# PEER gates in two passes of 64 expert rows instead of three, with gates stored ahead of the activations, in a two-layer encoder kernel

## The chip, the cores and the metric

The kernel runs on one core of a Trainium2 chip. The metric is the device time of one execution in microseconds (us); each figure below is a median of three executions, or one execution that the hardware profiler recorded. The engines are TensorE (PE in the rows; PEld is its weight load), VectorE (DVE), ScalarE (ACT), GpSimd (POOL) and SyncE (SP), which issues most DMA transfers.

## What is computed

Two encoder layers on 256 tokens of width 1024. Each layer is a token mixer (two attention branches), which the change does not touch, and a PEER block, which it does:

```python
def peer_ffn(x, w_query, sub_keys, expert_down, expert_up):
    # per head, product-key top-k over 128 x 128 experts; expert e adds g_e * v_e * gelu(u_e . x)
    def chunk(xc):                                    # PEER_CHUNK = 128 tokens, two chunks
        q = (xc @ w_query).reshape(128, 8, 2, half)
        s = einsum('thpk,pnk->thpn', q, sub_keys)
        sv, si = top_k(s, 16)
        cand = ...                                    # 16 x 16 sums and their expert numbers
        top_s, sel = top_k(cand, 16)
        eidx = take_along_axis(cidx, sel, axis=-1)    # 8 heads x 16 experts of each token
        g = softmax(top_s, axis=-1)
        u, vv = expert_down[eidx], expert_up[eidx]    # 16384 experts x 1024
        act = gelu(einsum('td,thkd->thk', xc, u))
        return einsum('thk,thkd->td', g * act, vv)
```

## The kernel before

**The PEER block as the kernel does it.** The 16384 experts are a grid of 128 rows i by 128 columns j. The kernel does not gather `expert_down`: it multiplies all 128 rows of it (one row is 128 experts, one *down unit*, D0 to D127, 24 matmuls of 256 columns) with all 256 tokens. Two units share a PSUM bank, the ScalarE applies Gelu to it, and the result stands in `act` (128 j, 128 i, 2 chunks, 128 tokens and one number). The *gates*, the softmax weights, are then multiplied into `act`, where an expert that a token did not pick gets zero. `expert_up` is read only where some token picked the expert: the rows of `act` are sorted into lists in DRAM, experts used by the first chunk alone, by both, by the second alone, and by none, and only the blocks of 128 experts up to a cap are read back, each with a gather of its 128 rows of `expert_up`. The other rows are taken whole, without sorting. A *block* is U0, U1, and so on; a block for one chunk is 6 matmuls of 512 columns, for both chunks 12.

**Precision.** Every weight tile `raw` is split into `wh` (ScalarE copy, L190) and `wl` (VectorE subtraction, L193), four of each in turn; a product is three matmuls. The copy of unit k+4 can start when TensorE is done with unit k. A block's slice of `act` is split too (L1214 and L1216), after the split of its `raw`.

**Lists.** `LISTS = [(0, 56, 46, 34, 11), (92, 36, 30, 22, 7)]` gives for each list its first row, its rows, and in blocks its cap, the end of the first chunk's and the start of the second chunk's. `WHOLE = (56, 36)` are the rows taken whole. `blocks_of` puts them in order: list 0, the whole rows, list 1.

**Gates.** `gate_lane` starts `gate_group` for each of the 32 groups of 8 tokens, in three passes, over the rows of list 0, the whole rows, and those of list 1 (`GATES`). A group builds on VectorE the one-hot rows `ej` (128 columns j, L1017), `ei` (w rows i, L1022) and `ag` (ei times the gate, in two halves, L1026), on ScalarE `el` (L1020), and on TensorE 16 matmuls per group for the gates (L1043) and, in the two passes of a list, 8 more that count which chunk uses which expert (L1039). VectorE then multiplies the gates from PSUM into `act` (L1053). This last step waits for the Gelu of the pass's last row, so the third pass cannot finish a group before all 128 rows are activated.

**From ranks to blocks.** When a pass of a list is through, `rank_lane` turns the counts into a place for every expert. `send_lane` then lets GpSimd write the list's rows out, one indirect DMA of 128 experts each (L1132), paced by waits on VectorE's splits: for list 0 every second send waits for a new split, for list 1 each. `read_back` (SyncE, L1169) reads a sorted block once all sends of its list have landed, and GpSimd gathers its `expert_up` rows (L1198).

**What sets the order.** Each engine runs a fixed order, written by `Lanes`: a planner that holds a clock for TensorE, VectorE and ScalarE and lets each lane (a Python generator) issue its next step when the planned time has come. TensorE's steps are the main loop; the gates, splits and Gelus are lanes that fill the other engines. The numbers in the `yield`s are planned costs. They order the instructions and do not hold them up on the chip, where only semaphores do.

## Time and profile before

| what | us |
|---|---|
| median of three executions (1909.34 to 1910.23) | 1909.83 |
| the profiled execution | 1909.23 |
| its span from first to last instruction | 1907.4 |
| down units of layer 1 on TensorE, first matmul to last | 247.1 to 657.7 |
| gates of layer 1 on TensorE | 400.1 to 767.6 |
| blocks of layer 1 on TensorE | 669.3 to 960.0 |
| down units of layer 2 | 1194.8 to 1605.4 |
| blocks of layer 2 | 1617.0 to 1903.2 |

All rows below are of the profiled execution. A row of the timeline starts with the start in us and the duration in us; "xN" is the number of like instructions merged into it, and a bracket tells how long the engine was idle before it and what ended that. Matmuls overlap, and so do instructions in a row on VectorE and ScalarE, so what one instruction costs its engine is the distance between two starts, which is less than its duration.

### The profile page before, as it was taken

Reading aid. Unit: us, or ns where it says so; the run is one execution under the profiler, and the core shown is the slowest. Engines: PE = TensorE matmul, PEld = TensorE weight load, DVE = VectorE, ACT = ScalarE, POOL = GpSimd, SP = SyncE. Lnnn points to the kernel's source line nnn. Section 1 sums busy time; section 2 is a strip of 40 time slices with the busy share of each in tenths; the row PEclk is TensorE's granted clock in tenths of the full one; section 3 lists DMA queues with packets and bytes.
Section 4 is the critical chain, followed back from the end, with each engine's and each line's share of the span. In section 5 each row is a group of like instructions: output and inputs, shape, how many; then the busy total and the mean of one; then the engine's idle time right before and its main releaser. Section 6 shows DMA issues by size and latency. Waiting matters only on the chain. (4 is left out here: it accounts for less than half of the span.)

```text
span 1907.4 us, 40308 instructions
## 1 busy us (share of the span) xinstructions
PE 1869.3 (98%) x15922; PEld 1695.4 (89%) x15922; DVE 1551.6 (81%) x3281; ACT 1109.0 (58%) x1550; POOL 383.6 (20%) x344
## 2 busy tenths in 40 slices
PE   8999999999999899999999999999999998999998
PEld 7889899999999878788778989999999998787886
DVE  6976899988988699755689778999889886996565
ACT  4665454556666577545646654455666665775454
POOL 0000000000054544335200000000000544534352
PEclk8999999999999999999999999999999998999999
DMA  7434455554467687877464354555544776778783
GB/s 254 155 110 159 155 177 190 177 176 145 155 207 222 214 261 233 269 235 263 163 230 140 110 179 141 178 184 182 168 149 148 222 220 228 249 239 259 205 291 129
DMA packets 122652, 370.74 MB, mean 194 GB/s; under 512 B 16080, under 2 KB 36432, under 8 KB 122448
## 3 DMA queue, kind: packets, MB, share of 16 engines
q1 hardware_dynamic: 91728, 264.00, 44.4%
q0 software_dynamic: 30720, 104.02, 15.5%
q8 instruction: 129, 2.11, 0.5%
q14 instruction: 75, 0.61, 0.1%
HBM read 342.60 MB, written 25.35 MB: 193 GB/s over the span
## 5 line engine op out<-in xcount | busy, mean ns | idle before, releaser
L190 ACT ACTIVATE wh<-raw 128x1024 fp32r<-128x1024 f32 x480 | 506.0, 1056 | 326.8 <-PE bank L1273 129.5
L193 DVE TENSOR_TENSOR wl<-raw,wh 128x1024 fp32r<-128x1024 f32 x480 | 582.0, 1219 | 135.9 <-ACT wh L190 132.9
L1272 PE MATMUL bank<-TT,wh 128*128 128x256 f32 x2048 | 585.3, 286 | 0.0
L1274 PE MATMUL bank<-TT,wl 128*128 128x256 f32 x2048 | 578.9, 283 | 0.0
L1273 PE MATMUL bank<-TT,wh 128*128 128x256 f32 x2048 | 578.6, 283 | 0.0
L1306 PE MATMUL bank<-wh,TT 128*128 128x512 f32 x1464 | 413.9, 400 | 7.5 <-PEq L1321 4.5
L1272 PEld LDWEIGHTS bank<-TT,wh 128*128 128x128 f32 x2048 | 387.3, 189 | 0.2
L1273 PEld LDWEIGHTS bank<-TT,wh 128*128 128x128 f32 x2048 | 386.0, 188 | 0.0
L1274 PEld LDWEIGHTS bank<-TT,wl 128*128 128x128 f32 x2048 | 385.2, 188 | 0.0
L1306 PEld LDWEIGHTS bank<-wh,TT 128*128 128x128 f32 x1464 | 273.2, 189 | 77.8 <-DVE TT L1216 8.2
L1132 POOL DMA_INDIRECT rows<-act,rank x184 | 199.1, 1082 | 512.4 <-DVE scr L1113 278.0
L1306 PE MATMUL bank<-wl,TT 128*128 128x512 f32 x732 | 232.6, 397 | 1.2 <-issue 1.2
L193 DVE TENSOR_TENSOR wl<-act,wh 128x1024 fp32r<-128x1024 f32 x132 | 161.2, 1223 | 82.1 <-ACT wh L190 80.0
L1020 ACT ACTIVATE el<-ej 128x1024 f16<-128x1024 f16 x192 | 193.5, 1046 | 57.1 <-DVE ej L1017 56.9
L190 ACT ACTIVATE wh<-act 128x1024 fp32r<-128x1024 f32 x132 | 139.3, 1057 | 107.3 <-PE bank L1306 103.2
L1224 ACT ACTIVATE act<-bank 128x512 f32<-128x512 f32 x128 | 76.6, 598 | 157.3 <-PE bank L1274 155.5
L1306 PEld LDWEIGHTS bank<-wl,TT 128*128 128x128 f32 x732 | 138.2, 189 | 33.4 <-DVE wl L193 0.3
L871 POOL IOTA act<- 128x128 uint32 x4 | 1.7, 437 | 804.6 <-PE bank L356 416.8
L1053 DVE TENSOR_TENSOR act<-act,bank 128x288 f32<-128x288 f32 (+1 forms) x192 | 93.3, 508 | 63.7 <-PE bank L1043 39.6
L436 PE MATMUL bank<-TT,wh 128*128 128x256 f32 x448 | 129.8, 290 | 1.5 <-ACT raw_ka L564 1.0
L438 PE MATMUL bank<-TT,wh 128*128 128x256 f32 x448 | 126.7, 283 | 0.0
L439 PE MATMUL bank<-TT,wl 128*128 128x256 f32 x448 | 126.5, 282 | 0.0
(249 smaller groups left out, 3039.9 us busy)
## 6 DMA issues: line engine op xcount, KB each, us to landing
raw<-in_downs_dram SPq DMA_DIRECT2D x256, 512.0 KB, 3.6
raw<-in_wts_dram SPq DMA_DIRECT2D x132, 512.0 KB, 3.7
act<-in_ups_dram SPq DMA_DIRECT2D x44, 512.0 KB, 4.9
raw<-in_ups_dram SPq DMA_DIRECT2D x28, 512.0 KB, 5.1
act<-rows SPq DMA_DIRECT2D x76, 129.0 KB, 3.8
act<-rows SPq DMA_DIRECT2D x76, 64.5 KB, 4.4
rows<-act,rank POOLq DMA_INDIRECT x184, 4.8
Sq<-in_rpb_dram SPq DMA_DIRECT2D x2, 876.0 KB
```

What stands on the lines that cost most here:

```text
L190: self.nc.scalar.activation(h, r, AF.Copy)
L193: self.splits.append(self.nc.vector.tensor_sub(lo, r, h.bitcast(F32)).ins.name)
L436: nc.tensor.matmul(o, wh, rh, start=first and i == 0 and pc == 0, stop=False, skip_group_check=True)
L438: nc.tensor.matmul(o, wh, rl, start=False, stop=False, skip_group_check=True)
L439: nc.tensor.matmul(o, wl, rh, start=False, stop=last and i == len(kcs) - 1 and pc == 1, skip_group_check=True)
L1020: nc.scalar.activation(el, ej, AF.Copy, scale=LOW)
L1053: nc.vector.tensor_mul(a, a, b[:, 0:8 * w].rearrange("p (t i) -> p i t", i=w))
L1132: snd = nc.gpsimd.indirect_dma_start(byrank[r], bass.IndirectOffsetOnAxis(ap=rank[:, i:i + 1], axis=0), afl[:, i * ROW:(i + 1) * ROW], None)
L1272: nc.tensor.matmul(o, lh, TT[:, :, 0, kc, :], start=kc == 0, stop=False)
L1273: nc.tensor.matmul(o, lh, TT[:, :, 1, kc, :], start=False, stop=False)
L1274: nc.tensor.matmul(o, ll, TT[:, :, 0, kc, :], start=False, stop=kc == 7)
L1306: nc.tensor.matmul(oacc[ch][hf], a, r[:, hf * 512:(hf + 1) * 512], start=first[hf] and a is lh and r is h, stop=last and a is ll)
```

## The change

1. **Two passes.** `GATES` is gone; `gate_group` now covers 64 rows in each of two passes, so 64 groups a layer in place of 96. A group has 16 gate matmuls of 64 columns (36 or 56 before) and always 8 counting matmuls, of 64 columns in the first pass (rows of list 0) and of 36 in the second (rows of list 1).
2. **Gates first or Gelu first.** A group no longer waits for the Gelu of its rows. Rows that are activated by then are multiplied on VectorE as before (L1059); for the rest the ScalarE stores the gates in `act` as they are (L1062). `gelu_lane` does the converse: for tokens whose gates are stored it applies Gelu in place in PSUM (L1244) and VectorE multiplies it into `act` (L1252), chunk by chunk; the other tokens are activated straight into `act` (L1249).
3. **Lists.** `LISTS = [(0, 64, 53, 39, 13), (92, 36, 30, 22, 7)]`, `WHOLE = (64, 28)`. A layer has 26 blocks for both chunks and 27 for one in list 0 (23 and 23 before), 28 whole rows (36), and list 1 as before: 180 products of a block with a chunk in place of 186, 111 splits in place of 112, 100 sends in place of 92.
4. **Sends.** Sends of list 0 are paced at 0.4 splits each and those of list 1 at 0.6; list 1 starts when every block of list 0 has been asked for. A send of list 0 no longer waits for the end of the gates of other rows, only for its own row and the rank.

```diff
-LISTS = [(0, 56, 46, 34, 11), (92, 36, 30, 22, 7)]
-WHOLE = (56, 36)
-GATES = [LISTS[0][:2] + (0,), WHOLE + (None,), LISTS[1][:2] + (1,)]
+LISTS = [(0, 64, 53, 39, 13), (92, 36, 30, 22, 7)]
+WHOLE = (64, 28)
...
+        cnts, counted, gates, gelus = {}, [0, 0], [0, 0], [0]
+
+        def gate_group(r, n, o):
...
+            i0, w = LISTS[r][:2]
+            p0 = 64 * r
...
             for t in range(8):
-                if r is not None:
-                    nc.tensor.matmul(cnts[r][:, (n // 16) * w:(n // 16 + 1) * w], ej[:, t // 2, :, t % 2],
...
+                nc.tensor.matmul(cnts[r][:, half * w:(half + 1) * w], ej[:, t // 2, :, t % 2],
+                                 ei[:, t // 2, i0 - p0:i0 - p0 + w, t % 2], start=counted[r] == 0 and t == 0,
+                                 stop=counted[r] == NG - 1 and t == 7, skip_group_check=True)
...
-            yield from lane_need([("gelu", (i0 + w) // 2 - 1)])
-            t = yield ("v", vcost(8 * w))
...
+            while gates[r] < n:
+                yield None
+            t = yield ("v", 0.35)
+            bv = b.rearrange("p (t i) -> p i t", i=64)
+            g = min(max(2 * gelus[0] - p0, 0), 64)
+            if g:
+                t = lanes.use("v", vcost(8 * g) - 0.35)
+                a = act[:, p0:p0 + g, half, t0:t0 + 8]
+                nc.vector.tensor_mul(a, a, bv[:, 0:g])
+            if g < 64:
+                t = max(t, lanes.use("s", scost(8 * (64 - g)), lanes.cur - 0.3))
+                nc.scalar.activation(act[:, p0 + g:p0 + 64, half, t0:t0 + 8], bv[:, g:64], AF.Copy)
...
         def send_lane(r):
...
-            yield from lane_need([("G", 2 * r), ("rank", r)])
+            yield from lane_need([("rank", r)])
+
+            while r and st.nd < up0 + len([x for x in seq if x[1] == 0]):
+                yield None
+            pace = len(st.splits) - 3.0
             for i in range(i0, i0 + w):
+                yield from lane_need([("row", i // 2)])
...
+                pace += (0.4, 0.6)[r]
...
         def gelu_lane(b, acc):
...
+            r, av = b // 32, acc.rearrange("p (a t) -> p a t", a=2)
+
+            g = 8 * gates[r]
+            if g:
+                nc.scalar.activation(av[:, :, 0:g], av[:, :, 0:g], AF.Gelu)
+            for c in range(2):
+                g0 = min(max(g - 128 * c, 0), 128)
+                a, ac = act[:, 2 * b:2 * b + 2, c], av[:, :, 128 * c:128 * c + 128]
+                if g0 < 128:
+                    nc.scalar.activation(a[:, :, g0:128], ac[:, :, g0:128], AF.Gelu)
+                if g0:
+                    t = max(t, lanes.use("v", vcost(2 * g0), lanes.cur))
+                    nc.vector.tensor_mul(a[:, :, 0:g0], a[:, :, 0:g0], ac[:, :, 0:g0])
```

**What it does to the order: VectorE in the second pass.** From the split of unit D110 to that of D112, before (L1017, L1022, L1026 build a group, L1053 multiplies gates into `act`):

```order
L193 TENSOR_TENSOR wl<-raw,wh 128x1024
L1022 TENSOR_TENSOR ei_2244<-iota_71,ijT 128x4x72
L1026 TENSOR_TENSOR ag_2246<-ei_2244,gT 128x4x72 x2
L1022 TENSOR_TENSOR ei_2245<-iota_71,ijT 128x4x72
L1026 TENSOR_TENSOR ag_2247<-ei_2245,gT 128x4x72 x2
L1053 TENSOR_TENSOR act<-act,bank_7694 128x36x8
L1053 TENSOR_TENSOR act<-act,bank_7699 128x36x8
L193 TENSOR_TENSOR wl<-raw,wh 128x1024
L1017 TENSOR_TENSOR ej_2240<-iota_71,ijT 128x1024
L1017 TENSOR_TENSOR ej_2241<-iota_71,ijT 128x1024
L193 TENSOR_TENSOR wl<-raw,wh 128x1024
```

and now, from the split of D109 to that of D111 (L1024, L1028 and L1019 build a group, L1059 multiplies gates into `act`, L1252 a Gelu from PSUM):

```order
L192 TENSOR_TENSOR wl<-raw,wh 128x1024
L1059 TENSOR_TENSOR act<-act,bank_7750 128x42x8
L1024 TENSOR_TENSOR ei_2244<-iota_71,ijT 128x512
L1028 TENSOR_TENSOR ag_2246<-ei_2244,gT 128x512 x2
L1019 TENSOR_TENSOR ej_2241<-iota_71,ijT 128x1024
L192 TENSOR_TENSOR wl<-raw,wh 128x1024
L1024 TENSOR_TENSOR ei_2245<-iota_71,ijT 128x512
L1028 TENSOR_TENSOR ag_2247<-ei_2245,gT 128x512 x2
L1252 TENSOR_TENSOR act<-act,bank_7774 128x2x88
L192 TENSOR_TENSOR wl<-raw,wh 128x1024
```

The multiplication of a fresh Gelu (L1252) now stands directly ahead of the split of D111; before, VectorE had no part in a Gelu.

**ScalarE at the same place**, before (L1020 makes `el`, L1224 is the Gelu of a bank, L190 the copy `wh`):

```order
L1020 ACTIVATE el_2242<-ej_2240 128x1024
L1020 ACTIVATE el_2243<-ej_2241 128x1024
L1224 ACTIVATE act<-bank_7275 128x4x128
L190 ACTIVATE wh<-raw 128x1024 x2
L1020 ACTIVATE el_2242<-ej_2240 128x1024
L1020 ACTIVATE el_2243<-ej_2241 128x1024
```

and now (L1022 makes `el`, L1062 stores gates, L189 is the copy `wh`):

```order
L189 ACTIVATE wh<-raw 128x1024
L1062 ACTIVATE act<-bank_7750 128x22x8
L1022 ACTIVATE el_2242<-ej_2240 128x1024
L189 ACTIVATE wh<-raw 128x1024
L1022 ACTIVATE el_2243<-ej_2241 128x1024
L1244 ACTIVATE bank_7774<-bank_7774 128x2x88
L1249 ACTIVATE act<-bank_7774 128x2x40
L1249 ACTIVATE act<-bank_7774 128x2x128
L189 ACTIVATE wh<-raw 128x1024
L1062 ACTIVATE act<-bank_7833 128x20x8
```

One Gelu has become three instructions. The second L1249 holds a wait for VectorE's L1252 on the same bank, and the copy `wh` of D111 stands right behind it.

**VectorE at the end of the down units**, before (the two last splits, then the third pass):

```order
L193 TENSOR_TENSOR wl<-raw,wh 128x1024 x2
L1053 TENSOR_TENSOR act<-act,bank_8605 128x36x8
L1053 TENSOR_TENSOR act<-act,bank_8610 128x36x8
L1053 TENSOR_TENSOR act<-act,bank_8874 128x36x8
L1053 TENSOR_TENSOR act<-act,bank_8875 128x36x8
L1017 TENSOR_TENSOR ej_2240<-iota_71,ijT 128x1024
L1017 TENSOR_TENSOR ej_2241<-iota_71,ijT 128x1024
L1022 TENSOR_TENSOR ei_2244<-iota_71,ijT 128x4x72
```

and now (from the split of block U0 to that of U2; L1229 splits a block's slice of `act`):

```order
L192 TENSOR_TENSOR wl<-raw,wh 128x1024
L1024 TENSOR_TENSOR ei_2245<-iota_71,ijT 128x512
L1028 TENSOR_TENSOR ag_2247<-ei_2245,gT 128x512 x2
L1059 TENSOR_TENSOR act<-act,bank_8864 128x62x8
L1019 TENSOR_TENSOR ej_2240<-iota_71,ijT 128x1024
L192 TENSOR_TENSOR wl<-raw,wh 128x1024
L1024 TENSOR_TENSOR ei_2244<-iota_71,ijT 128x512
L1028 TENSOR_TENSOR ag_2246<-ei_2244,gT 128x512 x2
L1059 TENSOR_TENSOR act<-act,bank_8941 128x62x8
L1252 TENSOR_TENSOR act<-act,bank_8931 128x2x128
L1252 TENSOR_TENSOR act<-act,bank_8931 128x2x72
L192 TENSOR_TENSOR wl<-raw,wh 128x1024
```

Before, the four multiplications behind the last split of a down unit waited for the last Gelu, with six groups of the third pass behind them; now the splits of the first blocks stand among the groups, and 7 groups are left for the time of the blocks, where 26 were.

## Rows read from the trace of the kernel before

**Rows 1.** The page, part 1: TensorE's matmuls, busy us, share, instructions.

```profile
PE 1869.3 (98%) x15922; PEld 1695.4 (89%) x15922; DVE 1551.6 (81%) x3281; ACT 1109.0 (58%) x1550; POOL 383.6 (20%) x344
```

**Rows 2.** Stretches: length, each engine's busy us, PEclk, DMA share, GB/s.

```profile
490.00:520.00 30.00, 30.00 (x378) 29.72 (x378) 26.65 (x48) 18.45 (x21) 0.00 (x0) 1.00 0.48 158
...
731.00:761.00 30.00, 30.00 (x297) 24.02 (x296) 29.73 (x63) 22.68 (x32) 14.13 (x12) 1.00 0.75 233
```

**Rows 3.** Timeline of TensorE: 24 matmuls of a down unit, 6 of a block.

```profile
329.88 0.28 PE L1272 MATMUL bank<-TT,wh 128*128 128x256 f32 x1
...
332.76 0.28 PE L1272 MATMUL bank<-TT,wh 128*128 128x256 f32 x1
...
800.78 1.10 PE L1306 MATMUL bank<-wh,TT 128*128 128x512 f32 x4
...
802.19 1.09 PE L1306 MATMUL bank<-wh,TT 128*128 128x512 f32 x4
```

**Rows 4.** Timeline of TensorE: first matmul of three gate bursts, first behind each.

```profile
485.52 0.20 PE L1039 MATMUL bank<-ei,ej 128*128 128x56 f16 x1
...
486.17 0.37 PE L1272 MATMUL bank<-TT,wh 128*128 128x256 f32 x1
...
567.47 0.19 PE L1043 MATMUL bank<-ag,ej 128*128 128x36 f16 x1
...
568.29 0.36 PE L1272 MATMUL bank<-TT,wh 128*128 128x256 f32 x1
...
711.36 0.20 PE L1039 MATMUL bank<-ei,ej 128*128 128x36 f16 x1
...
712.57 0.48 PE L1306 MATMUL bank<-wh,TT 128*128 128x512 f32 x1
```

**Rows 5.** Line L1306 from the last down unit: us, PE, PEld, PEclk, DMA, GB/s.

```profile
657.70:684.80 27.10, 13.57 (x48) 9.83 (x49) 0.81 0.83 296
1605.40:1633.10 27.70, 14.12 (x49) 10.25 (x50) 0.75 0.80 283
```

**Rows 6.** Timeline of VectorE: a group of the first pass, and the last down unit.

```profile
485.14 1.23 DVE L193 TENSOR_TENSOR wl<-raw,wh 128x1024 fp32r<-128x1024 f32 x1
486.37 0.62 DVE L1053 TENSOR_TENSOR act<-act,bank 128x448 f32<-128x448 f32 x1
486.91 0.38 DVE L1022 TENSOR_TENSOR ei<-iota,ijT 128x448 f16<-128x448 f16 x1
...
487.94 0.69 DVE L1017 TENSOR_TENSOR ej<-iota,ijT 128x1024 f16<-128x1024 f16 x1
488.54 1.22 DVE L193 TENSOR_TENSOR wl<-raw,wh 128x1024 fp32r<-128x1024 f32 x1
...
658.62 0.82 DVE L1053 TENSOR_TENSOR act<-act,bank 128x288 f32<-128x288 f32 x2 [9.35 <-ACT act L1224]
```

**Rows 7.** Timeline of ScalarE in the second pass.

```profile
596.50 1.06 ACT L190 ACTIVATE wh<-raw 128x1024 fp32r<-128x1024 f32 x1 [2.11 <-PE bank L1273]
597.46 1.99 ACT L1020 ACTIVATE el<-ej 128x1024 f16<-128x1024 f16 x2
```

**Rows 8.** Groups by line and shape: ScalarE, 256 elements; busy us, mean ns.

```profile
L1214 ACT ACTIVATE TT<-act 128x256 fp32r<-128x256 f32 x146 | 58.5, 400 | 0.0
```

**Rows 9.** Timeline of GpSimd: sends of list 0, then the first gather.

```profile
534.02 1.16 POOL L1132 DMA_INDIRECT rows<-act,rank  x1 [139.00 <-DVE scr L1113]
...
541.34 1.91 POOL L1132 DMA_INDIRECT rows<-act,rank  x1 [0.30 <-issue]
...
551.25 0.96 POOL L1132 DMA_INDIRECT rows<-act,rank  x1 [0.30 <-issue]
...
646.64 1.34 POOL L1132 DMA_INDIRECT rows<-act,rank  x1 [0.30 <-issue]
653.12 0.99 POOL L1198 DMA_INDIRECT raw<-in_ups_dram,act  x1 [5.14 <-DMA act<-rows]
```

**Rows 10.** The page, part 6: loads of whole rows, KB each, us to landing.

```profile
raw<-in_ups_dram SPq DMA_DIRECT2D x28, 512.0 KB, 5.1
```

More of the change, by code (lines that the diff above doesn't have):

```diff
@@ L1036, in gate_group @@
             yield ("p", 0.75)
+            half, t0 = n // 16, 8 * (n % 16)
             for t in range(8):
[L1038 to L1041 removed]
+                nc.tensor.matmul(cnts[r][:, half * w:(half + 1) * w], ej[:, t // 2, :, t % 2],
+                                 ei[:, t // 2, i0 - p0:i0 - p0 + w, t % 2], start=counted[r] == 0 and t == 0,
+                                 stop=counted[r] == NG - 1 and t == 7, skip_group_check=True)
@@ L1042, in gate_group @@
                 for k, e in enumerate((ej, el)):
-                    nc.tensor.matmul(b[:, t * w:(t + 1) * w], e[:, t // 2, :, t % 2],
+                    nc.tensor.matmul(b[:, t * 64:(t + 1) * 64], e[:, t // 2, :, t % 2],
                                      ag[:, k, t // 2, :, t % 2], start=k == 0, stop=k == 1)
-            counted[g] += 1
-            if counted[g] == NG and r is not None:
+            counted[r] += 1
+            if counted[r] == NG:
                 lanes.add(rank_lane(r, cnts[r]), after=lanes.cur)
@@ L1059, in gate_lane @@
+            if gates[r] == NG:
+                for k in range(32 * r, min(gelus[0], 32 * r + 32)):
+                    done["row", k] = t
         def gate_lane():
             yield from lane_need(["idx"])
-            for g in range(len(GATES)):
+            for r in range(2):
                 for n in range(NG):
                     o = yield from buf_take("oh")
-                    lanes.add(gate_group(g, n, o), after=lanes.cur)
+                    lanes.add(gate_group(r, n, o), after=lanes.cur)
@@ L1204, in split_rows @@
             if seq[n - up0][1] is None:
-                yield from lane_need([("G", 1)])
+                yield from lane_need([("row", seq[n - up0][2] // 2)])
             while n not in stage:
@@ L1222, in gelu_lane @@
         def gelu_lane(b, acc):
+            while gelus[0] < b:
+                yield None
             t = yield ("s", scost(512))
-            nc.scalar.activation(act[:, 2 * b:2 * b + 2, :, 0:HALF - 1],
-                                 acc.rearrange("p (a c t) -> p a c t", a=2, c=2), AF.Gelu)
+            r, av = b // 32, acc.rearrange("p (a t) -> p a t", a=2)
[10 more added lines that the diff above has]
+                    nc.vector.tensor_mul(a[:, :, 0:g0], a[:, :, 0:g0], ac[:, :, 0:g0])
+            lanes.cur = max(lanes.cur, t)
             give(acc, "a")
-            done["gelu", b] = t
+            gelus[0] += 1
+            if gates[r] == NG:
+                done["row", b] = t
         for ch in range(2):
```

43 lines of the change are left out of this document (15 added, 28 removed).

## The prediction

> **What bounds the kernel now.** I read the page's busy shares first: TensorE 1869.3 us, 98% of the span, VectorE 81%, ScalarE 58% [rows 1]. A busy TensorE can still be a waiting one, so next come the distances between its matmuls. A down unit's 24 matmuls take 2.88 us, 0.120 each, and a block's 6 take 1.41 us, 0.235 each [rows 3], and a gate group stands between two units without a hole [rows 4]. So from the first down unit to the last block TensorE's own work sets the time, and what leaves its queue leaves the time. There is one exception: at the end of the down units, 48 block matmuls and 8 gate groups need 27.1 us in layer 1 and 27.7 in layer 2 with the clock granted at 0.81 and 0.75 of full speed, part of it at the lower level [rows 5]. There VectorE sat 9.35 us behind the last Gelu [rows 6], its queue holding the third pass in order. Last the slack beside TensorE: VectorE is busy 26.65 of 30 us in the first pass, and 29.73 of 30 later among the blocks, still without holding TensorE up [rows 2].
>
> **Gates.** Bursts cost, from their first matmul to the first one behind [rows 4]: 24 matmuls at 56 columns 0.65 us (27.1 ns each), 32 at 36 columns (two groups) 0.82, 48 at 36 (two groups) 1.21. A layer has 32 groups of the first, 16 of the second, 16 of the third sort: 20.8 + 13.1 + 19.4 = 53.3 us. Now 64 groups of 24. At 64 columns the price is unseen; from 25.4 ns at 36 and 27.1 at 56 I go on to 27.7, with 25.4 (columns free) and 29.5 (the slope doubled) as ends. First pass 32 x 24 x 27.7 = 21.3; second, with 8 counting matmuls at 36 columns, 32 x (16 x 27.7 + 8 x 25.4) = 20.7; together 42.0. That removes 11.3 us per layer, 22.6 in all, 18 to 27 between the ends. All of it lies on TensorE's path.
>
> The rows show 25.4 ns at 36 columns and 27.1 at 56, a weak slope. [...]
>
> **Blocks.** 180 products in place of 186, 36 matmuls fewer per layer at 0.235 us [rows 3]: 8.5 us, 16.9 in all.
>
> **The stall at the end of the down units.** In rows 5 the work is 48 x 0.235 = 11.3 us and 8 x 0.61 = 4.9 of gates; 27.1 - 16.2 = 10.9 us are wait and low clock. Layer 2, with one matmul more, 27.7 - 16.4 = 11.3. The third pass that held VectorE's queue is gone, and the splits of the first blocks are now ahead of the last Gelu's product, so 22.2 us go, unless something else is late there. Candidates are the next two points.
>
> **The hand-off that is added.** In the second pass each pair of down units has a chain that was not there: VectorE multiplies part of the Gelu (L1252), then ScalarE's second Gelu instruction, which waits for that, then the copy `wh` of the next unit behind it in ScalarE's queue, then VectorE's split, with nothing between on VectorE. Its price: 0.40 us for 256 elements [rows 8], 1.06 for the copy [rows 7], less 0.1 where they overlap, and about 0.1 for the signals, so VectorE idles some 1.5 us per pair. Is there room? VectorE's prices by distance of starts [rows 6]: split 1.14 to 1.23, `ei` and both `ag` 1.03 at 56 columns, so 1.15 at 64, `ej` 0.60, gates into `act` 0.54 for 448 elements. Walk the order shown for D109 and D110 from the moment the copy of D109 is there: split 1.2, gates (336 elements) 0.4, `ei` and `ag` 1.15, `ej` 0.6, in all 3.35. ScalarE meanwhile waits for the gates at 1.6, stores its share (0.3), makes `el` (0.94 [rows 7]) and copies D110 by 4.0, so VectorE waits 0.65. Then split 1.2, `ei` and `ag` 1.15, the product 0.3, and the chain of 1.5: 8.1 us. TensorE needs 2 x 2.88 and one or two groups of 0.65, 6.4 to 7.1. Walked in the same way, the ten pairs from D107 to D127 take 7.2, 8.1, 7.5, 8.1, 8.3, 6.4, 8.2, 7.9, 7.5 and 6.6, 75.8 us against 20 x 2.88 + 14 x 0.65 = 66.7 on TensorE; D98 to D107 come out some 5 us over. So VectorE loses about 14 us per layer in the second pass. Its lead pays for half: ScalarE waits for TensorE to free a `wh` four units back [rows 7], so a split ends three units (8.6) and a group or two (1.0) less copy and split (2.3), or about 7 us, before its use. What is left, 7 us, reaches TensorE. Then, without a lead, the first 20 blocks: VectorE has 20 splits, 17 splits of `act`, 8 times `ei` and `ag`, 7 `ej`, 9 gate products and the second rank, about 50 us, against 30 x 1.41 + 8 x 0.65 = 47.5 on TensorE: 2.5 more. I take 9.5 per layer, 19 in all. The lower end is 1 per layer (ScalarE always early, lead never spent), the upper 16 (the 14 in full and 2.5). The walk decides for the middle, since every term in it but the signals has a row.
>
> [...]
>
> **Sends.** Eight more sends per layer on GpSimd, which has no part in the rest; what counts is when the last one lands. The first send followed the rank at 534.02, twelve sends followed each other at 17.23 / 11 = 1.57 us, the last ended at 647.98, the first gather began 5.1 us later [rows 9]; then 5.1 to landing by the nearest row [rows 10], copy and split 2.3. Now the rank comes 32 units before the blocks: 32 x 2.88 + 23 x 0.65 = 107, and 7 of the waits above make 114 us; 64 sends at 1.57 are 100.5, and with 12.5 for the rest 113. It just fits, and nothing is charged; the bound is 0 to 4 us per layer. List 1 has 28 whole rows, 79 us, for 36 sends, which at 1.57 are 57. Its last rows are gathered no later than before. Nothing is charged.
>
> **Neither gain nor loss.** ScalarE loses 32 `el` copies per layer and gains the stores and split Gelus; at 18.45 of 30 us [rows 2] it has the room, apart from the order above. One split per layer less is covered by TensorE.
>
> **Sum.** 1909.2 (the profiled execution, 0.6 below the median, which I leave out) - 22.6 - 16.9 - 22.2 + 19 = 1866.5. I say **1866 us**.
>
> **Rivals.**
> 1. *The hand-off is hidden.* ScalarE would have to reach its second Gelu before VectorE is idle and the lead of 7 us to outlast the pass. For it: VectorE stood at 29.73 of 30 us among the blocks and TensorE did not wait [rows 2]. Against it: there the lead was full and ScalarE waited for nothing of VectorE's. 1909.2 - 61.7 + 2 = 1849.5, with 4 us either way for the price at 64 columns: 1846 to 1857.
> 2. *Hand-off in full, or the sends a little late.* 16 us per layer, or 9.5 and 4 to 6 for sends at 1.65: 1875 to 1890. For it: sends of 1.91 us stand among those of 0.96 [rows 9].
> 3. *Slower: the sends starve the first blocks.* All 64 land before the first sorted block can be read. If they took 1.91 + 0.30 each, the longest in rows 9, they would need 141 us, the first block would be 28 us late in each layer, and the sum would be 1866.5 + 56 = 1922. It turns slower where a send's mean passes 1.57 + 21.4 / 64 = 1.90 us. Rows 9 speak against it: beside the same kinds of VectorE work twelve sends averaged 1.57. [...]
> 4. *The change doesn't do what it says:* if the picks overflowed the caps, the branch that makes up for them would load both lists again. From the reference's own picks list 0 needs 6671 and 6681 places of 53 x 128 = 6784, so I give it nothing.
>
> **Chances.** My forecast (1857 to 1875) 0.50, rival 1 0.29, rival 2 0.15, rival 3 0.04, and 0.02 for something that leaves the time within 0.2%, about what a measurement of this kernel can tell from no change. So faster 0.94, same 0.02, slower 0.04. The range takes in most of the first three: 1848 to 1884.
>
> **What would show it.** Gate bursts of 24 at 0.65 to 0.68 us. In the second pass ScalarE's L1249 waiting for VectorE's L1252 once per pair, VectorE's split waiting for `wh` about 1.5 us behind each L1252, and TensorE waiting for `wl` from about D115 on, 5 to 9 us in all; if TensorE has no hole before D127, rival 1 holds. At the start of the blocks 1 to 5 us of holes, the clock near full. GpSimd's last send 15 us or more before the first block; if the first gather is what the first block waits for, it is rival 2 or 3. I am wrong at the root if TensorE's bursts or blocks come out at other prices than those of rows 3 and 4.

## The result, and the profile after

The changed kernel takes **1889.81 us** (median of 4 runs, 1887.28 to 1891.15) against 1909.95 of the kernel before on the same chip: a ratio of 0.9893, 95% interval 0.9876 to 0.9911. That is 20 us (1.1%) faster, where 43 were forecast and 1848 was the lower and 1884 the upper end. The profiled execution has 1889.17 us and a span of 1887.4.

The page of the changed kernel, part 1, answers [rows 1]: TensorE's share is the same, its busy time 23 us less.

```profile
PE 1846.0 (98%) x14826; PEld 1672.6 (89%) x14826; DVE 1493.7 (79%) x3017; ACT 1075.3 (57%) x1710; POOL 423.9 (22%) x374
```

Stretches of the changed kernel, columns as in [rows 2]: the first pass, the second pass, and a place among the blocks.

```profile
490.00:520.00 30.00, 30.00 (x373) 29.66 (x372) 26.72 (x45) 16.70 (x23) 0.00 (x0) 1.00 0.50 158
600.00:630.00 30.00, 28.57 (x332) 27.36 (x331) 22.79 (x42) 17.84 (x31) 23.31 (x22) 1.00 0.81 238
...
731.00:761.00 30.00, 30.00 (x130) 24.12 (x129) 21.26 (x31) 18.84 (x30) 18.57 (x14) 1.00 0.90 299
```

The second row is the one to look at. In the second pass TensorE has idle time, while VectorE, which ought to be what holds it up, is busy for only 22.79 of 30 us. Neither engine is full, so one waits for the other in turns. The third row shows that VectorE is no longer near its limit among the blocks (21.26 in place of 29.73).

Timeline of TensorE, as in [rows 4]: a gate burst of the first pass, one of the second without a wait, and one of the second with a wait; each with its first matmul and the first of the next unit.

```profile
492.40 0.20 PE L1041 MATMUL bank<-ei,ej 128*128 128x64 f16 x1
...
493.13 0.36 PE L1302 MATMUL bank<-TT,wh 128*128 128x256 f32 x1
...
571.28 0.19 PE L1041 MATMUL bank<-ei,ej 128*128 128x36 f16 x1
...
571.97 0.36 PE L1302 MATMUL bank<-TT,wh 128*128 128x256 f32 x1
...
627.20 0.18 PE L1041 MATMUL bank<-ei,ej 128*128 128x36 f16 x1
627.66 0.20 PE L1045 MATMUL bank<-ag,ej 128*128 128x64 f16 x1 [0.28 <-DVE ag L1028]
...
628.62 0.36 PE L1302 MATMUL bank<-TT,wh 128*128 128x256 f32 x1
```

The three take 0.73, 0.69 and 1.42 us. The first two are prices; they were forecast at 0.66 and 0.65. The third is a wait, and it lies inside the burst: the counting matmul has begun, and the gate matmul behind it needs `ag`, which VectorE has only just made.

All waits of TensorE's matmuls that the changed kernel shows from 545 to 660 us, and the two `ag` of the third burst; then, in the kernel before, the two `ag` of each of the two groups of the second pass whose burst starts at 567.47 [rows 4], and the first gate matmul of the second of them:

```profile
PE bank L1045 <- ACT el L1022: 1.1, 5, 0.3
PE bank L1045 <- DVE ag L1028: 1.1, 4, 0.3
...
627.18 0.76 DVE L1028 TENSOR_TENSOR ag<-ei,gT 128x512 f16<-128x512 f16 x2
...
566.01 0.53 DVE L1026 TENSOR_TENSOR ag<-ei,gT 128x288 f16<-128x288 f16 x2
...
566.79 0.53 DVE L1026 TENSOR_TENSOR ag<-ei,gT 128x288 f16<-128x288 f16 x2
...
567.89 0.18 PE L1043 MATMUL bank<-ag,ej 128*128 128x36 f16 x1
```

Before, the later `ag` of each group ends 0.93 and 0.57 us ahead of the group's first gate matmul; now it ends 0.28 us behind it (627.94 and 627.66). In five of the nine waits ScalarE's `el` came last, at most 0.2 us behind `ag`, and no wait is for `wl`. The view counts only what a wait leaves uncovered by the matmuls before it; by the distances of starts the bursts lose more (the table at the end of this section).

Waits of VectorE and ScalarE in the changed kernel from 545 to 660 us (line, what it waited for, us in total, times, longest).

```profile
DVE wl L192 <- ACT wh L189: 19.0, 20, 1.4
...
DVE act L1252 <- ACT act L1249: 1.8, 5, 0.4
...
ACT act L1062 <- DVE act L1059: 27.9, 17, 3.0
ACT act L1249 <- DVE act L1252: 15.3, 14, 2.5
```

Both halves of the hand-off are there. ScalarE's second Gelu instruction waits for VectorE's product, and VectorE's split waits for the copy `wh` that stands behind that Gelu. One pair from close by, VectorE first, then ScalarE:

```profile
643.08 0.41 DVE L1252 TENSOR_TENSOR act<-act,bank 128x256 f32<-128x256 f32 x1
643.92 0.19 DVE L1252 TENSOR_TENSOR act<-act,bank 128x32 f32<-128x32 f32 x1 [0.43 <-ACT act L1249]
644.86 1.23 DVE L192 TENSOR_TENSOR wl<-raw,wh 128x1024 fp32r<-128x1024 f32 x1 [0.76 <-ACT wh L189]
...
641.62 0.40 ACT L1244 ACTIVATE bank<-bank 128x288 f32<-128x288 f32 x1
643.52 0.36 ACT L1249 ACTIVATE act<-bank 128x224 f32<-128x224 f32 x1 [1.51 <-DVE act L1252]
643.78 1.05 ACT L189 ACTIVATE wh<-raw 128x1024 fp32r<-128x1024 f32 x1
```

VectorE multiplies, waits 0.43 us for ScalarE, multiplies again, and waits 0.76 for the copy. ScalarE had been ready 1.51 us before. That is 1.2 us of idle VectorE in this pair, and (19.0 + 1.8) / 14 = 1.5 in the mean of the 14 pairs of the window whose Gelu is divided in this way, the waits at the splits of both units of a pair counted; 1.5 were forecast.

Line L1336 from the last down unit to the place behind the first 48 block matmuls, in both layers, answers [rows 5]; then one row of TensorE's timeline from that stretch:

```profile
670.40:693.90 23.50, 13.87 (x48) 10.63 (x49) 0.85 0.79 267
1608.20:1630.50 22.30, 12.63 (x48) 9.76 (x49) 0.92 0.78 268
...
677.19 0.19 PE L1041 MATMUL bank<-ei,ej 128*128 128x36 f16 x1 [2.54 <-DVE ei L1024]
```

The stretch is shorter (27.1 and 27.7 before), but the clock is still below full in it, and TensorE still waits there (2.54 us for VectorE's `ei` ahead of L1041).

GpSimd, as in [rows 9]: the first send of list 0, the last, the first gather.

```profile
551.77 2.04 POOL L1152 DMA_INDIRECT rows<-act,rank  x1 [156.72 <-DVE miss L1124]
...
640.65 0.96 POOL L1152 DMA_INDIRECT rows<-act,rank  x1 [0.30 <-issue]
659.88 1.49 POOL L1211 DMA_INDIRECT raw<-in_ups_dram,act  x1 [18.27 <-DMA act<-rows]
```

64 sends follow each other at (640.65 - 551.77) / 63 = 1.41 us, and the last ends 37 us ahead of the first block at 679.0. The sends cost nothing here.

**Where the time went.** For a ledger I take the distances of the unit starts on TensorE and subtract the work in them: 0.1198 us for a matmul of a down unit, 0.2345 for one of a block, and 25.4, 27.1 and 30.7 ns for a gate matmul of 36, 56 and 64 columns. The matmuls of the ranks, the same number in each kernel, are taken off too (1.4 us from D48 to D127, 1.1 from U8 to U64, 0.9 behind it in layer 1). What is left over, in us per layer (layer 1, layer 2; D127 is the last down unit; U counts here products of a block with a chunk, 6 matmuls each, so U8 stands behind the first 48 block matmuls; 0.08 per gate burst is a steady remainder and no wait):

| stretch | before | changed | gelus_first_3 (below) |
|---|---|---|---|
| D48 to D127 | 3.8, 3.8 | 14.1, 14.3 | 4.5, 4.5 |
| D127 to U8 | 10.9, 11.5 | 6.6, 5.4 | 2.6, 2.6 |
| U8 to U64 | 2.0, 1.9 | 1.2, 2.4 | 2.6, 2.5 |
| U64 to the last block | 8.2, 3.3 | 8.9, 4.2 | 8.3, 4.0 |
| sum | 24.9, 20.5 | 30.8, 26.3 | 18.0, 13.6 |

The work itself fell by 8.4 us of blocks and 7.5 of gates per layer, 32 in all; the leftovers grew by 5.9 and 5.8, about 12. 32 - 12 is the 20 us that were measured. The stall at the end of the down units shrank, as forecast, though not to nothing; more than that came back before it, inside the down units.

### The profile page after: what moved, and what is told of

Its sections match the earlier page's. It is cut to its first block, busy times and chain, and to the rows that moved or that the text cites. A ratio compares the mean times of both kernels' runs of the same rounds, so it can differ in the third digit from the quotient of the medians.

```text
span 1887.4 us, 37955 instructions
## 1 busy us (share of the span) xinstructions
PE 1846.0 (98%) x14826; PEld 1672.6 (89%) x14826; DVE 1493.7 (79%) x3017; ACT 1075.3 (57%) x1710; POOL 423.9 (22%) x374
## 5 line engine op out<-in xcount | busy, mean ns | idle before, releaser
L189 ACT ACTIVATE wh<-raw 128x1024 fp32r<-128x1024 f32 x478 | 504.3, 1058 | 254.4 <-PE bank L1336 76.3
L1304 PE MATMUL bank<-TT,wl 128*128 128x256 f32 x2048 | 577.1, 282 | 0.0
L1336 PE MATMUL bank<-wh,TT 128*128 128x512 f32 x1416 | 397.9, 400 | 8.3 <-PEq L1351 5.9
L1304 PEld LDWEIGHTS bank<-TT,wl 128*128 128x128 f32 x2048 | 385.0, 188 | 0.0
L1336 PEld LDWEIGHTS bank<-wh,TT 128*128 128x128 f32 x1416 | 266.0, 189 | 75.0 <-issue 6.7
L1152 POOL DMA_INDIRECT rows<-act,rank x200 | 220.4, 1102 | 374.0 <-DVE miss L1124 313.6
L1336 PE MATMUL bank<-wl,TT 128*128 128x512 f32 x708 | 225.5, 398 | 0.0
L189 ACT ACTIVATE wh<-act 128x1024 fp32r<-128x1024 f32 x132 | 139.7, 1060 | 120.0 <-PE bank L1336 113.0
L1249 ACT ACTIVATE act<-bank 128x256 f32<-128x256 f32 (+7 forms) x240 | 79.8, 369 | 173.1 <-PE bank L1304 121.5
L1336 PEld LDWEIGHTS bank<-wl,TT 128*128 128x128 f32 x708 | 134.1, 189 | 32.7
L1022 ACT ACTIVATE el<-ej 128x1024 f16<-128x1024 f16 x128 | 133.2, 1050 | 19.9 <-DVE ej L1019 19.3
L1211 POOL DMA_INDIRECT act<-in_ups_dram,act x96 | 117.3, 1222 | 101.4 <-DVE TT L1229 88.0
```

The lines of the kernel that those rows point to most:

```text
L189: self.nc.scalar.activation(h, r, AF.Copy)
L1022: nc.scalar.activation(el, ej, AF.Copy, scale=LOW)
L1152: snd = nc.gpsimd.indirect_dma_start(byrank[r], bass.IndirectOffsetOnAxis(ap=rank[:, i:i + 1], axis=0), afl[:, i * ROW:(i + 1) * ROW], None)
L1211: nc.gpsimd.indirect_dma_start(w, None, ups_rows, bass.IndirectOffsetOnAxis(ap=num, axis=0), element_offset=l * 16384 * D)
L1304: nc.tensor.matmul(o, ll, TT[:, :, 0, kc, :], start=False, stop=kc == 7)
L1336: nc.tensor.matmul(oacc[ch][hf], a, r[:, hf * 512:(hf + 1) * 512], start=first[hf] and a is lh and r is h, stop=last and a is ll)
```

## The experiments

The theory after the result was: VectorE and ScalarE wait for each other at each pair of down units in the second pass (the hand-off), which makes `ag` late, and 64 columns cost more than assumed in the prediction. The rivals were that VectorE has too much work there, that the groups stand too early in TensorE's queue, and that sends or blocks are late.

The chips that the experiments ran on were of two sorts. On one the kernel before takes 1909 us; on the other 1957 to 1959, with an idle time that the first doesn't have (last section). Each result is told with the time of the kernel before beside it.

**Both Gelu instructions first** (gelus_first). The products come behind them, so ScalarE doesn't wait for VectorE within a pair; the work is the same.

```diff
             for c in range(2):
...
                 if g0 < 128:
                     nc.scalar.activation(a[:, :, g0:128], ac[:, :, g0:128], AF.Gelu)
+            for c in range(2):
...
                 if g0:
...
                     nc.vector.tensor_mul(a[:, :, 0:g0], a[:, :, 0:g0], ac[:, :, 0:g0])
```

> The changed kernel (1889.8 us) with one thing reordered: of a pair of down units ScalarE does both of its Gelu instructions (L1249) first and VectorE's products (L1252) come behind them, so ScalarE never waits for VectorE inside a pair. The work is the same. Theory 'hand-off': in the changed kernel TensorE waits some 7.4 us per layer from D98 to D127 and some 7.5 us more from D127 to U32 because VectorE stands idle about 1.2 us per pair, first for ScalarE's second Gelu and then for the copy wh behind it. Then the idle time per pair falls to about 0.5 us and half or more of the 15 us per layer goes: 1870 to 1880. Rival 'work': VectorE simply has more to do there than TensorE's units last, and the hand-off only moves its idle time about: 1887 to 1892. Rival 'order': gate groups stand too early in TensorE's queue whatever VectorE does: TensorE still waits some 0.3 us for ag at each group of the second pass, 1885 to 1892.

Measured 1956.96 us against 1959.1, ratio 1.0001 (0.9974 to 1.0028). That can't be compared with the first result, since it was the other chip: TensorE lost some 35 us per layer from D94 to D118 in another way. What could be read was the stretch ahead of the sends: D58 to D68 had 0.6 us left over in place of 2.2 to 2.5.

**The store first as well** (store_first).

```diff
+            if g < 64:
...
+                nc.scalar.activation(act[:, p0 + g:p0 + 64, half, t0:t0 + 8], bv[:, g:64], AF.Copy)
             if g:
...
                 nc.vector.tensor_mul(a, a, bv[:, 0:g])
-            if g < 64:
...
-                nc.scalar.activation(act[:, p0 + g:p0 + 64, half, t0:t0 + 8], bv[:, g:64], AF.Copy)
```

> The kernel of gelus_first with a second thing reordered: of a gate group ScalarE's store of the rows not yet activated (L1062) comes ahead of VectorE's product of the activated rows (L1059), so ScalarE doesn't wait for VectorE there either (in the changed kernel it waits about 2 us at each store of the second pass). Theory 'hand-off': these waits hold the copies wh behind them up as well, and 2 to 8 us more go than in gelus_first: 1864 to 1876. Rival: ScalarE has the room for them, 18 of 30 us busy, and nothing changes against gelus_first (within 2 us). Third: VectorE now waits for ScalarE's store and loses as much as ScalarE gains, 3 us or more slower than gelus_first.

1958.46 us, 1.0009 (0.9986 to 1.0032), beside the run above; nothing could be told apart on this chip.

**No mixing** (pass_after_pass).

```diff
-            while gates[r] < n:
+            while gates[r] < n or 2 * gelus[0] < p0 + 64:
                 yield None
```

> The changed kernel without the mixing: a gate group's result waits until all Gelus of its pass are done, as before the change, so there are no products L1252, no stores L1062 and no hand-off, but the whole second pass of 32 groups lies behind the last Gelu. Theory 'hand-off': TensorE's waits from D98 to D127 (7.4 us per layer) are gone; in their place the stall at the end of the down units that the kernel before had (10.9 us per layer, at a clock of 0.8) comes back, and more of it, since 32 groups of VectorE's work (2.3 us each with 64 columns) stand among the first blocks in place of 6: 1890 to 1930. Rival 'work': the waits from D98 to D127 stay as they are. A time under 1885 would say that the mixing itself loses more than the stall it removes.

1970.87 us, 1.0064 (1.0042 to 1.0087), on the same chip. It was run again on the other.

**The lists alone** (three_passes_new_lists).

```diff
-LISTS = [(0, 56, 46, 34, 11), (92, 36, 30, 22, 7)]
-WHOLE = (56, 36)
+LISTS = [(0, 64, 53, 39, 13), (92, 36, 30, 22, 7)]
+WHOLE = (64, 28)
```

> The kernel before with the lists alone changed (64 and 36 rows, 28 whole); gates still in three passes (64, 28 and 36 columns) that wait for their Gelus, and sends paced as before. Terms: 180 products in place of 186 a layer, 2 x 8.5 us less; 64 columns in the first pass, 0.738 us a burst in place of 0.652, 2 x 2.75 us more; the other passes as before. So 1909.9 - 16.9 + 5.5 = 1898.5. Rival: the 8 more sends a layer at 1.57 us make the first sorted blocks up to 4 us late in each layer: 1899 to 1907. If the blocks were not on the path the time would be 1910 or more.

2180.97 us, 1.1133 (1.11 to 1.1165): missed by far. The planner now put all 32 groups of the third pass ahead of the first block, which began 114 us behind the last down unit, and in the midst of it next to nothing moved over the DMA (columns as in [rows 2]):

```profile
700.00:760.00 60.00, 34.16 (x677) 24.33 (x678) 50.69 (x141) 29.59 (x28) 0.00 (x0) 0.51 0.01 2
```

So the run prices no list, and what held the loads up was not followed further. Taken alone, the lists don't fit the old order. What it does confirm is the price of a block: among the later blocks 504 matmuls in a row take 118.08 us, 0.234 each.

**Once more on one chip, with the changed kernel beside them** (changed_again, gelus_first_2, store_first_2).

> The changed kernel once more, unaltered, beside the next three on one chip. In the four runs before, the kernel before took 1959 us in place of 1910, and in gelus_first TensorE had some 35 us of idle time per layer between D94 and D118, within bursts and with no data outstanding, while the sends ran. If that belongs to the chip, the changed kernel shows it too there (its ratio to the kernel before then near 1.00, like gelus_first); on a chip without it the ratio is again near 0.989 and TensorE's idle time lies at the first gate matmul behind VectorE's ag, 0.3 us a group.

> The kernel of gelus_first (both of ScalarE's Gelu instructions of a pair ahead of VectorE's products), against the changed kernel on one chip. In the first run TensorE's excess from D58 to D68, ahead of the sends, was 0.6 us per layer in place of 2.2 to 2.5, and from D118 to D127 0.4 in place of 2.9. Theory 'hand-off': against changed_again it is 8 to 20 us faster (1870 to 1881 where that has 1889). Rival 'work': within 3 us of changed_again.

> The kernel of store_first (ScalarE's store of the rows not yet activated ahead of VectorE's product, too), on the same chip. Theory 'hand-off': 2 to 8 us faster than gelus_first_2. Rival 'room': within 2 us of it.

It was the other chip again (before 1957.65). changed_again 1948.29 us, 0.9956 (0.9939 to 0.9972); gelus_first_2 1942.16, 0.9921 (0.9895 to 0.9948); store_first_2 1942.06, 0.9898 (0.9865 to 0.9932). The changed kernel gains only about half as much there. The reordering, from which 8 to 20 us were expected, has a median 6 us lower, less than the spread of either kernel (1942.5 to 1950.9 and 1930.4 to 1949.9), so it isn't told apart from nothing. That VectorE catches up while TensorE stands still for the other reason would explain it, but is not shown: from D118 to D127 changed_again has 0.9 and 2.4 us left over, where the first trace has 2.9 in both layers, and from D58 to D68 as much as the first.

**The price of a column** (price_of_columns).

```diff
+            wg = (64, 60, 58, 56, 52, 48, 40, 32)[n % 8]
...
-                for k, e in enumerate((ej, el)):
-                    nc.tensor.matmul(b[:, t * 64:(t + 1) * 64], e[:, t // 2, :, t % 2],
...
+                for c0, c1 in ((0, wg), (wg, 64))[:1 + (wg < 64)]:
+                    for k, e in enumerate((ej, el)):
+                        nc.tensor.matmul(b[:, t * 64 + c0:t * 64 + c1], e[:, t // 2, :, t % 2],
...
```

> The changed kernel with each gate product over 64 columns cut into two matmuls, of w and 64 - w columns, where w goes through 64 (uncut), 60, 58, 56, 52, 48, 40 and 32 from group to group; the sums are the same, with 16 matmuls more a burst. It prices a matmul by its columns: uncut bursts again at 0.738 us in the first pass (30.7 ns each). [...] Theory 'line', as the prediction had it: 27.7 at 64 and 27.1 at 56, so all pairs within 1 ns of 52. [...] The time itself is some 15 us above the changed kernel.

Timeline of TensorE, first pass: the first matmul of four bursts, each with the first of the unit behind it (line L1304 here). They are uncut, 58 + 6, 56 + 8 and 52 + 12.

```profile
512.40 0.20 PE L1042 MATMUL bank<-ei,ej 128*128 128x64 f16 x1
...
513.14 0.36 PE L1304 MATMUL bank<-TT,wh 128*128 128x256 f32 x1
...
520.90 0.20 PE L1042 MATMUL bank<-ei,ej 128*128 128x64 f16 x1
...
522.03 0.36 PE L1304 MATMUL bank<-TT,wh 128*128 128x256 f32 x1
...
527.87 0.20 PE L1042 MATMUL bank<-ei,ej 128*128 128x64 f16 x1
...
528.95 0.36 PE L1304 MATMUL bank<-TT,wh 128*128 128x256 f32 x1
...
531.19 0.20 PE L1042 MATMUL bank<-ei,ej 128*128 128x64 f16 x1
...
532.25 0.36 PE L1304 MATMUL bank<-TT,wh 128*128 128x256 f32 x1
```

The first takes 0.733 us, the same in all 8 of its kind. The cut ones take 1.062 us at 32 + 32 and 52 + 12, 1.067 at 40 + 24, 1.074 at 48 + 16, 1.078 at 56 + 8, 1.125 at 58 + 6 and 1.130 at 60 + 4. Less 8 counting matmuls at 0.733 / 24 = 30.5 ns and shared among 16 pairs that is 51.1, 51.4, 51.9, 52.1, 55.1 and 55.4 ns a pair. If the small piece costs half of 51.1, an estimate that the run doesn't show by itself, a matmul costs 25.6 ns up to 52 columns, 26.5 at 56 (27.1 uncut in [rows 4]), 29.5 at 58, 29.8 at 60 and 30.5 at 64. The theory 'line' misses: it has all pairs within 1 ns of 52, and they go from 51.1 to 55.4. The price is level up to about 52 columns, and the pair costs 3 ns more at 58 + 6 than at 56 + 8. Why is open. The time of the run, 1973.05 us, is a single one on the other sort of chip (changed_again: 1948.29) and says nothing beside this.

**Sends held back** (sends_late, then with the two reorderings).

```diff
-            while r and st.nd < up0 + len([x for x in seq if x[1] == 0]):
+            while gelus[0] < 64 or r and st.nd < up0 + len([x for x in seq if x[1] == 0]):
                 yield None
```

> The changed kernel with its sends of list 0 held back until the last Gelu, so that none runs beside the down units; TensorE then stands still between the last down unit and the first sorted block, some 90 to 110 us per layer, which the next two kernels have as well. It takes away the idle time that belongs to the sends on this chip (some 30 us per layer from D94 to D118, in the middle of bursts). Theory 'sends': from D98 to D127 no idle time is left that ends with no data, and the excess of the first trace of the changed kernel is back: about 9 us per layer from D98 to D127, with TensorE waiting at the first gate matmul behind ag. If the idle time stays, it isn't the sends.

> The kernel of sends_late with both Gelu instructions of a pair ahead of VectorE's products. Theory 'hand-off': the excess from D98 to D127 falls from about 9 us per layer to 2 to 4 (steady cost 1.7), and the whole is 10 to 16 us shorter than sends_late, as far as the sends, which start with the last Gelu, pass it on. Rival 'work': the excess stays at 8 to 10.

> The kernel of sends_late_gelus_first with ScalarE's store ahead of VectorE's product as well. Theory 'hand-off': the two gate groups behind the last down unit wait no more (excess from D127 to the first block's place 1 us in place of 4), and the whole is a further 2 to 6 us shorter than sends_late_gelus_first. Rival 'room': within 1 us of it.

These ran on the first sort of chip (before 1909.09). sends_late 2026.2 us, sends_late_gelus_first 2005.86, sends_late_store_first 2005.6. The first reordering takes 20 us off, more than the 10 to 16 expected, and the second adds nothing to it. From D98 to D127 6.5 us are left over in each layer of the first kernel (9.1 in the changed one), 1.5 in the other two, which is the steady remainder. No send of list 0 ran beside the down units, and TensorE waited all the same; so 5 of the 7.5 us per layer aren't the sends' doing. What took the other 2.6 away is open: VectorE's order between D102 and D127 also changed a little. What the sends do on the other sort of chip could not be tested here.

**The changed kernel, the reorderings and no mixing, on the first sort of chip** (before 1909.39).

> The changed kernel unaltered, as the measure for the next three on their chip. Where the kernel before has 1909 to 1910 us, 1887 to 1891 again; where it has 1957 to 1959, 1943 to 1951.

> The kernel of gelus_first, on the chip of changed_3. With the sends held back the same reordering brought 20 us (2026.2 to 2005.9), 7 us per layer of it from D48 to D127. Theory 'hand-off': where the kernel before has 1909 us, this one has 1868 to 1876, 14 to 20 us less than changed_3. Rival: the 20 us came from the stretch that only the held-back sends opened, and here it is 1880 or more.

> The kernel of store_first, on the chip of changed_3. With the sends held back the store ahead of the product brought nothing (2005.9 and 2005.6), but that stretch hid the groups behind the last down unit, which waited 4.3 us per layer in the changed kernel, 3.6 to 5.4 in gelus_first_2 and 1.1 in store_first_2. Theory 'end of the down units': 4 to 9 us less than gelus_first_3. Rival 'room': within 2 us of it.

> The kernel of pass_after_pass (gate results wait for all Gelus of their pass; no hand-off, the whole second pass behind the last Gelu), on the chip of changed_3. Theory 'the stall of the kernel before was VectorE's queue behind the last Gelu': from D98 to D127 next to no excess, and behind D127 a stall longer than the 10.9 us per layer of the kernel before, 15 to 30 us. The whole 1895 to 1930 where the kernel before has 1909. If it is below changed_3, the mixing itself was the loss.

| kernel | us | ratio to before, 95% interval |
|---|---|---|
| changed_3 | 1888.58 | 0.9891, 0.9875 to 0.9908 |
| gelus_first_3 | 1861.1 | 0.9749, 0.9733 to 0.9765 |
| store_first_3 | 1862.08 | 0.9753, 0.9737 to 0.9769 |
| pass_after_pass_2 | 1933.54 | 1.0132, 1.0115 to 1.0149 |

VectorE's products moved behind ScalarE's second Gelu bring 27.5 us, more than the 14 to 20 expected and more than the whole change did, and give the fastest kernel of this study. In gelus_first_3 the stretch of the second pass, its waits on VectorE from 545 to 660, and one pair (ScalarE, then VectorE; the product is L1255 here) read so:

```profile
600.00:630.00 30.00, 30.00 (x358) 29.73 (x357) 25.70 (x46) 18.64 (x32) 23.61 (x22) 1.00 0.86 253
...
DVE wl L192 <- ACT wh L189: 7.6, 15, 0.9
...
624.54 0.41 ACT L1244 ACTIVATE bank<-bank 128x272 f32<-128x272 f32 x1
624.98 0.37 ACT L1249 ACTIVATE act<-bank 128x240 f32<-128x240 f32 x1
625.25 1.05 ACT L189 ACTIVATE wh<-raw 128x1024 fp32r<-128x1024 f32 x1
...
625.39 0.50 DVE L1255 TENSOR_TENSOR act<-act,bank 128x256 f32<-128x256 f32 x2 [0.43 <-ACT act L1249]
626.33 1.23 DVE L192 TENSOR_TENSOR wl<-raw,wh 128x1024 fp32r<-128x1024 f32 x1 [0.45 <-ACT wh L189]
```

ScalarE now goes straight from its Gelus to the copy, the products run beside that copy, and VectorE waits for `wh` 7.6 us in the stretch instead of 19.0. It does more in the same 30 us (25.70 in place of 22.79), and from 545 to 660 us no wait of TensorE is left. The work is the same: both kernels run 3017 instructions on VectorE, 1494 us, and 1710 on ScalarE. That refutes the rival 'work', and 'order' with it, since TensorE waits for neither `ag` nor `el` any more. The stretches of changed_3 against gelus_first_3, in us per layer (layer 1, layer 2): D48 to D68 2.0 and 2.2; D68 to D98 nothing; D98 to D127 7.6 and 7.6; D127 to U8 4.3 and 4.2; U8 to U64 -1.6 and -1.5; from there to the end 1.4 and -0.2. The sum is 13.7 and 12.3, 26.0 in all, and the two profiled spans differ by 1888.2 - 1862.0 = 26.2.

store_first_3 stands within 1 us of gelus_first_3: ScalarE's 2 us waits at the stores (L1062) cost the kernel nothing. That is 'room'.

pass_after_pass_2 has no wait in the down units (3.7 us left over from D0 to D127, all steady), but the first block starts 42.6 us behind D127:

```profile
644.80:687.40 42.60, 12.73 (x218) 11.39 (x217) 16.19 (x35) 8.56 (x11) 29.05 (x31) 0.60 0.40 132
...
648.24 1.29 DVE L1059 TENSOR_TENSOR act<-act,bank 128x512 f32<-128x512 f32 x2 [9.07 <-ACT act L1249]
...
ACT wh L1227 <- DMA act<-rows: 16.5, 1, 16.5
...
675.13 0.96 POOL L1152 DMA_INDIRECT rows<-act,rank  x1 [0.30 <-issue]
```

The second row is that of [rows 6] again: VectorE waits 9.07 us for the last Gelu (9.35 there), because its queue holds a product that needs it. So the wait that the changed kernel had lost comes back with the old order, as the reading of the stall says. It isn't the whole of the 42.6 us, though: here the last send also falls at 675 us, and ScalarE's first copy of a sorted block (third row) waits 16.5 us for the rows to be read back. The time is above the range that was expected, and the mixing, even with its hand-off, is worth 45 us against this.

## Why the prediction was wrong

The sum came to 1866.5; the profiled execution took 1889.2, 22.7 us more. Three of its terms were mis-sized, and one of them, the hand-off, also had a step of its mechanism wrong.

- **What bounds the kernel:** right. TensorE's queue sets the time, and its leftovers add up to the difference.
- **Gates, -22.6:** mis-sized, -15 measured. The bursts are 0.73 and 0.69 us; 64 columns cost 30.5 to 30.7 ns, above the upper end of 29.5. I drew a line through 25.4 at 36 and 27.1 at 56 and went on 8 columns past the last row. The failed step is "I go on to 27.7": there is a step in the price just behind that row (52.1 ns a pair at 56 + 8, 55.1 at 58 + 6 in price_of_columns), so two rows on one side of it could tell nothing of the other. This is 7.5 us of the miss.
- **Blocks, -16.9:** right; 36 matmuls fewer per layer, and among the later blocks of either kernel 540 in a row take 126.5 us and 504 take 118.1.
- **The hand-off, +19:** the chain was right, the size too small: 26.0 us by changed_3 against gelus_first_3, 13 per layer, inside the bounds of 1 to 16. What was missed in size is the stretch: I charged the second pass and the first 20 blocks. The same chain stands at the pairs up to D66, where the first pass multiplies, 2 us per layer, 4.2 of the 7 us that were missed. The second pass cost 7.6 per layer where 7 were forecast, and behind D127 it was 4.3 up to U8 less 1.6 up to U64, 2.7 beside 2.5; the last 1.2 us stand behind U64 (1.4 in layer 1, -0.2 in layer 2) and are not explained.
- **The step of the hand-off that failed in its mechanism** is "Its lead pays for half". The lead of 7 us is that of the splits. The gate operands have none such: in the trace of the kernel before, the last `ag` of a group ends 0.5 to 1.0 us ahead of TensorE's use in most groups of the second pass. So TensorE waited for `ag` and `el` (L1045), not for `wl`, from about D102 on, while the splits still led by 3.4 us in the mean. What TensorE needs first from a late engine is the operand with the least lead, not the one with the most. That the second pass came to 7.6 us beside 7 is in part luck: the splits' lead fell from 8.0 us (D90 to D98) to 3.4 (D104 to D127), so it paid 4.6 and not 7, but with the 7.5 that reached TensorE VectorE lost 12 us and not the 14 of the walk. The 0.1 us for the signals had no row; in the pair shown above L1249 starts 0.03 us behind the end of L1252, and the split 0.03 behind that of the copy.
- **The stall at the end of the down units, -22.2:** right in its cause (VectorE's queue behind the last Gelu, as pass_after_pass_2 shows), too high in size. The failed step is "so 22.2 us go": all of it was struck. Even in gelus_first_3, with no hand-off and the clock at 1.00 there, 2.6 us per layer stay in that stretch, two gate groups still waiting for `ei` and `ag` among them. With small rises elsewhere (0.7 from D48 to D127, where there are more bursts, 0.6 from U8 to U64) that makes some 8 us.
- Together 7.5 + 7 + 8 are the 22.7 us but for rounding.
- **Sends, nothing charged:** right; they came at 1.41 us, not 1.57. VectorE was less busy beside them (22.79 of 30 us from 600 to 630, 25.96 before), and a send itself took 1.10 us in the mean, 1.11 before.
- **Rivals:** in its time the result lies where rival 2 does (1875 to 1890), but not by its road: with the hand-off as measured, and all else as forecast, the sum is 1873.5, and late sends played no part. The gates and the stall make up the rest. What rival 1 would come to, the hand-off hidden, is gelus_first_3: 1861, where 1846 to 1857 were worked out with the too low price of the columns and all of the stall struck.
- **Slips in the sums,** none of which moves the forecast: at 25.4 ns the gates gain 29 us, not 27; the slope doubled from 56 columns on is 28.5 ns at 64, not 29.5; rival 1's 4 us either way end at 1854, not 1857; in rival 3 the first block would be 40 us late, not 28, since the 12.5 us behind the sends were left out.
- **What would show it:** ScalarE's L1249 waiting for L1252 and VectorE's split waiting for `wh` came as named; TensorE waiting for `wl` didn't, and the place where it waits for `ag` wasn't on the list. The clock at the blocks was 0.85 and 0.92, not near full.

Why ScalarE has to wait at all: L1249 and L1252 read the same PSUM bank, and the kernel's waits put one behind the other. In the changed kernel that wait comes to 15.3 us, 14 times, from 545 to 660 us. No run here let the two go without it, so what that would do was not tried; gelus_first only turns the order round, so that ScalarE goes first, whose copy VectorE needs next.

## What to carry to other kernels

Where two engines take turns at one buffer, let the engine first that others wait for, and all its turns in one go: here that order alone was worth 27 us on the first sort of chip. When pricing an engine that falls behind, look for each thing the bound engine takes from it and use the smallest lead. And a price for a size that no row shows should not be drawn from rows on one side of it alone, when a single run of cut matmuls can measure it.

## What the runs showed of the hardware that I had not expected

**A step in the price of a matmul.** In price_of_columns, one run, with the clock granted at 1.00 from 470 to 500 us, a gate matmul (128 rows of f16) costs 30.5 ns at 64 columns, and the two pieces of a cut one together 51.1 ns at 32 + 32 and at 52 + 12, 52.1 at 56 + 8 and 55.1 at 58 + 6. With the small piece at half of 51.1, my estimate from the first of these pairs, that is 25.6 ns up to 52 columns, 26.5 at 56 and 29.5 at 58. Passes of 56 columns, at 27.1 ns in [rows 4], stood just below the step.

**Two sorts of chip.** On one the kernel before took 1957 to 1959 us in place of 1909. Two chips were of this sort, each seen at one time only, so it may as well be a condition that a chip was in. There TensorE stands idle in the middle of bursts, and the profile shows no operand that is outstanding (in gelus_first 13 times at L1045, 9.8 us). Waits of TensorE in gelus_first on that chip, 550 to 665 us, the three longest rows; then the stretch 555 to 665 of the changed kernel, on that chip (changed_again) and on the first:

```profile
PE bank L1045 <- issue: 9.8, 13, 1.8
PE bank L1041 <- issue: 2.9, 6, 1.2
PE bank L1307 <- issue: 2.8, 6, 0.7
...
555.00:665.00 110.00, 94.32 (x961) 90.00 (x960) 65.78 (x120) 53.28 (x90) 65.46 (x62) 0.86 0.59 183
...
555.00:665.00 110.00, 106.47 (x1227) 103.16 (x1226) 84.67 (x155) 64.56 (x111) 72.09 (x66) 1.00 0.74 224
```

"issue" means that the profile shows nothing that it waited for. The holes lie almost all in the stretches in which GpSimd sends rows and shortly behind them: in gelus_first they come to 20.0 us from 540 to 700 us, all of it from 550 to 665, and the sends go from 550.4 to 666.4. The granted clock is 0.86 from 555 to 665 us in changed_again; on the first chip there is none of these holes (no wait of TensorE on "issue" from 400 to 720 us in the changed kernel). That the sends cause them is not shown, since the kernels with the sends held back ran on a chip without the holes. Sends alone don't make them: in pass_after_pass, on a chip with the holes, 40 sends run beside D102 to D126 of layer 1 and TensorE loses nothing (busy 60.00 of 60 us from 540 to 600, where it begins), while in layer 2 the same order loses 12 us from D104 to D108. It stays open.
